# A transformer layer on one core: pre-norm weight applied behind the transposes, zeros through TensorE first, some masks by VectorE, a new order

## The chip, the core and the metric

The kernel runs on one core of a Trainium2 chip. A core has five engines with a queue of instructions each: TensorE (PE, matrix products and transposes), VectorE (DVE), ScalarE (ACT), GpSimd (POOL) and SyncE (SP, which here issues all DMAs). They run side by side and wait for each other by semaphores. TensorE reads SBUF and writes PSUM, which has eight banks of 128 x 512 float32. The metric is the device time of one execution in microseconds.

## The reference

One layer over 1024 tokens of width 1024, all in float32:

```python
h = rms_norm(x, norm_pre_g[i])          # x * rsqrt(mean(x*x) + EPS) * g
proj = h @ w_in[i]
# sb_q, sb_k, sb_v, sb_g, c_q, c_kv, k_rope, mla_g = split(proj)
# 8 heads of stick-breaking attention (strictly causal), head norm, times silu(sb_g)
# 8 heads of latent attention (low-rank q and kv, rotary key), head norm, times silu(mla_g)
y = concat([sb_y, mla_y]) @ w_out[i]
x = x + rms_norm(y, norm_post_g[i])
x = x + rms_norm(p[i] @ w_ple[i], ple_norm_g[i]) * sigmoid(x @ w_ple_gate[i] + b_ple_gate[i])
```

## The kernel before

Tokens come in eight tiles of 128 rows (x0 to x7). Every operand of a product is split into a high and a low part of the type fp32r, and a product of two operands is three TensorE products (high x high, high x low, low x high) summed in one PSUM bank.

**The head.** `HEAD` lists the first loads: four quarters of the weight of v (v0 to v3, each loaded and split by `load_split`), the tiles x0, x1, x2, and the pre-norm weight (g0, one row of 4 KB). Two products with a row of ones spread the weight over the 128 partitions, and ScalarE copies it to `gb["pre"]`. `x_norm(t)` squares and sums a tile (ScalarE), forms the mean (VectorE) and the power -1/2 (GpSimd), and multiplies the tile by both the power and the weight. `x_tr(t)` transposes it, four blocks of 128 x 128 to a bank, and `split` writes the high part (`hh`, ScalarE) and the low part (`hl`, VectorE). `token_proj(t)` then makes v for the tile: eight blocks kb with three products each; quarter i of the weight serves kb 2i and 2i+1. `xv_gen(t)` puts these together and loads x(t+3). The four first tiles are done ahead of everything else.

**The middle.** `SEQ` lists sixteen pairs of units: head pair c (0 to 3 stick-breaking, 4 to 7 latent), half s of the queries, and in each pair e = 0, 1. `sb_rows` makes the scores of four blocks of 128 queries: a product, a mask added on TensorE by a product of `eye` and `mask` (bf16, 128 columns), and a second product into the same bank; ScalarE reads the bank twice for two sigmoids. `Weaver` mixes projections (`FILL0`) into the units at `RATES`. `TAIL` lists the steps of the output projections at the end.

**The order.** Nothing is issued as it is written. `Recorder` records each operation with its dependences and a cost; `schedule` replays them through a model of the engines (`cost`, `LAT`) and takes, for each engine, the ready operation of lowest priority; `issue` emits the program in that order. The priority is `turn`, the operation's place in the program plus the first number of its piece in the table `SHIFT`; the second number ranks the requests for buffers. `R.piece` begins a new piece. `R.bias` shifts a stretch (`URGENT` for the head, `AHEAD` for scores). `FLIP` moves single operations between VectorE and GpSimd or ScalarE, `SPLITS` (read by `choice`) whole kinds of them between VectorE and GpSimd. Since all instructions are emitted in `issue`, the profile gives nearly all of them one line, L730; they are told apart by tiles: u and f are the two pools of SBUF slots, t and a the PSUM banks (five and three), h the large buffers, among them `hh` and `hl`.

Of the kernel before, what the change touches and what calls it, by code (L numbers as in the profile page):

```python
# [12 lines left out]
F32 = mybir.dt.float32  # L13
# [34 lines left out]
def f(ap):  # L48
# [6 lines left out]
TAIL = ("o4", "w1", "w2", "o5", "a4", "o6", "w3", "x1", "x0", "x2", "e4", "a0", "e0", "a6", "x3", "e6", "a2", "e2")  # L55
RATES = (4.934, 9.256, 4.735, 4.518, 3.1, 1.436, 0.789, 0.703, 2.078, 0.654, 0.413, 0.788, 0.259, 0.582, 0.786, 1.784)
URGENT = 56
EARLY = 4
LATER = 5
SEQ = ((0, 0), (1, 0), (6, 0), (4, 0), (7, 0), (2, 0), (0, 1), (3, 0), (3, 1), (2, 1), (5, 0), (7, 1), (5, 1), (4, 1), (1, 1), (6, 1))  # L60
FILL0 = ("x4", "x5", "l0", "x6", "x7", "q1", "c0", "b1", "r3", "t0", "lrv0", "g3", "rope0", "r0", "r1", "g4", "q2", "r2", "q3", "g6", "g0", "g1", "g2", "g7", "ple0", "g5")
# [4 lines left out]
SPLITS = (1, 0, 0, 1, 0, 1, 1, 1, 0, 1, 1, 1, 1, 1, 0, 1, 1, 0, 1, 0, 1, 1, 1, 0, 0, 1, 1, 1, 0, 0, 0, 1, 0, 0, 0, 1, 0, 0, 1, 0, 0, 1, 1)  # L66
HEAD = ("v0", "x1", "x0", "g0", "v3", "v1", "v2", "x2")
# [265 lines left out]
class Recorder:  # L333
# [127 lines left out]
    def cost(self, eng, op, args, kw, outs, aps, spaces):  # L461
        n = max(self.elems(a) for a in aps)
        ps = any(k == "psum" for _, k in spaces)
        if eng == "PE":
# [3 lines left out]
            if aps[1].dtype == BF16:  # L468
                return n * 0.305
# [47 lines left out]
    def schedule(self):  # L517
# [32 lines left out]
        dma_free = 0.0  # L550
        flight, room = [], 0
        port_free = 0.0
        table = None
        clock = {}

        why = self.why = {}
# [176 lines left out]
def block_kernel(ctx, tc, x, p, positions, norm_pre_g, w_in, q_norm_g, w_uq, kv_norm_g, w_ukv,  # L733
# [196 lines left out]
    gb = {}  # L930
# [857 lines left out]
```

## Time and profile before

| | |
|---|---|
| time, median of 3 runs | 773.64 us (772.73 to 775.02) |
| profiled execution: time, span | 774.4 us, 772.6 us |
| TensorE, VectorE, ScalarE, GpSimd busy | 98%, 81%, 50%, 45% |
| DMA traffic over the span | 148.69 MB, mean 192 GB/s |
| granted TensorE clock, mean | 0.998 |

The span runs from the first to the last instruction. A busy TensorE is not TensorE at its peak: ends of products are modelled, so a long row of products is best priced by its length over its count. A row of the chain of work gives start, length and what ran; a row of the groups gives count, then busy time and mean length in ns, then the idle time of the engine ahead of it and what ended that; a row of the timeline adds the engine and, in brackets, the idle time ahead.

### The profile page before, as it was taken

How to read it: one execution, taken by the hardware profiler on the slowest of the kernel's cores; microseconds unless marked ns; L12 is line 12 of the kernel's file. 1: busy time of each engine (PE TensorE's matmuls, PEld its weight loads, DVE VectorE, ACT ScalarE, POOL GpSimd, SP SyncE). 2: the span in 40 equal slices, each digit the busy share in tenths (PEclk: the TensorE clock that was granted, in tenths of full speed). 3: DMA queues.
4: the chain of work that ended last, by engine and by line, in shares of the span. 5: the costliest groups of instructions: out<-in, count | busy, mean ns of one | idle time of the engine just before them, and what ended most of it. 6: DMA issues, size and time to landing. Idle time of an engine off the chain costs nothing.

```text
span 772.6 us, 11778 instructions
## 1 busy us (share of the span) xinstructions
PE 754.5 (98%) x3912; PEld 621.5 (80%) x3912; DVE 624.1 (81%) x1184; ACT 384.9 (50%) x898; POOL 346.6 (45%) x315
## 2 busy tenths in 40 slices
PE   6999999999999999999999899999999999999997
PEld 4887889878788878888788788888888888778886
DVE  5876334499867877788888899999899998888996
ACT  6315123333443586565646768776776642433211
POOL 4445111102312258878884712342275114468664
PEclk9999999999999999999999999999999999999999
DMA  9644460269995844566356588686734475172242
GB/s 329 201 171 139 145 213 5 77 218 354 330 341 190 275 155 143 167 206 189 110 184 225 187 290 260 216 302 223 240 116 154 166 254 178 60 268 87 94 150 82
DMA packets 101966, 148.69 MB, mean 192 GB/s; under 512 B 7441, under 2 KB 55057, under 8 KB 101906
## 3 DMA queue, kind: packets, MB, share of 16 engines
q1 hardware_dynamic: 101906, 147.95, 57.4%
q8 instruction: 31, 0.51, 0.3%
q14 instruction: 29, 0.24, 0.1%
HBM read 101.26 MB, written 46.66 MB: 191 GB/s over the span
## 4 chain that ended last, share of the span: by engine, by line
PE 84%; DVE 7%; DMA 4%; ACT 2%; issue 1%; POOL 1%; SPq 1%; POOLq 0%; ACTq 0%; DVEq 0%
PE a L730 58%; PE t L730 26%; DVE u L730 4%; DVE f L730 2%; ACT u L730 1%; DMA u<-k_d 1%; DMA u<-in_w_ple_gate_dram 1%; DMA u<-q_d 1%; DMA u<-in_x_dram 1%; DMA f<-in_positions_dram 1%; DMA q_d<-f 1%; SPq L730 1%; DVE nm L730 1%; ACT f L730 0%; POOL u L730 0%
## 5 line engine op out<-in xcount | busy, mean ns | idle before, releaser
L730 POOL TENSOR_TENSOR u<-u,u 128x512 f32<-128x512 f32 (+16 forms) x134 | 200.5, 1512 | 153.3 <-DVE u L730 64.0
L730 PE MATMUL a<-h,f 128*128 128x512 f32 x864 | 242.1, 405 | 0.0
L730 PEld LDWEIGHTS a<-h,f 128*128 128x128 f32 x864 | 155.2, 189 | 26.8 <-DVE f L730 0.6
L730 DVE TENSOR_TENSOR u<-t,u 128x512 fp32r<-128x512 f32 (+4 forms) x284 | 150.6, 556 | 13.7 <-ACT u L730 10.0
L730 PE MATMUL t<-u,u 128*128 128x512 f32 (+4 forms) x580 | 154.4, 370 | 1.9 <-DMA u<-q_d 0.5
L730 PE MATMUL a<-u,u 128*128 128x512 f32 (+2 forms) x524 | 136.7, 371 | 0.5 <-DVE u L730 0.5
L730 PE MATMUL t<-ident,u 128*128 128x128 f32 x792 | 125.8, 276 | 2.4 <-DVE u L730 2.4
L730 ACT ACTIVATE u<-t 128x512 f32<-128x512 f32 (+5 forms) x208 | 91.0, 509 | 67.7 <-PE t L730 57.8
L730 PEld LDWEIGHTS t<-u,u 128*128 128x128 f32 x580 | 103.4, 189 | 23.2 <-DVE u L730 4.3
L730 ACT CAST u<-t 128x512 fp32r<-128x512 f32 (+3 forms) x187 | 85.6, 495 | 71.0 <-PE t L730 35.3
L730 PE MATMUL a<-h,u 128*128 128x512 f32 (+1 forms) x492 | 118.3, 390 | 0.4 <-DVE u L730 0.4
L730 PEld LDWEIGHTS t<-ident,u 128*128 128x128 f32 x792 | 97.8, 142 | 24.9 <-DVE u L730 7.0
L730 PEld LDWEIGHTS a<-h,u 128*128 128x128 f32 x492 | 90.0, 188 | 21.3 <-issue 1.0
L730 PEld LDWEIGHTS a<-u,u 128*128 128x128 f32 x524 | 93.1, 188 | 17.2 <-DVE u L730 2.2
L730 ACT ACTIVATE u<-t,nms 128x384 f32<-128x384 f32 (+4 forms) x96 | 55.3, 581 | 42.3 <-DVE nms L730 35.3
L730 DVE TENSOR_TENSOR_SCAN u<-u 128x64 f32<-128x64 f32 (+6 forms) x64 | 59.1, 934 | 20.6 <-ACT u L730 20.4
L730 DVE TENSOR_TENSOR u<-u,u 128x512 f32<-128x512 f32 (+13 forms) x91 | 73.2, 820 | 2.0 <-ACT u L730 1.1
L730 DVE TENSOR_TENSOR u<-a,u 64x512 f32<-64x512 f32 (+4 forms) x75 | 47.8, 649 | 15.6 <-ACT u L730 9.7
L730 DVE TENSOR_REDUCE nm<-t 128x1 f32<-128x384 f32 (+4 forms) x96 | 51.6, 545 | 2.1 <-PE t L730 1.3
L730 POOL TENSOR_TENSOR rs<-ms,nhalf 128x8 f32<-128x8 f32 x16 | 27.7, 1731 | 57.0 <-DVE ms L730 37.5
L730 ACT ACTIVATE f<-a 128x512 bf16<-128x512 f32 (+3 forms) x64 | 34.3, 538 | 36.7 <-PE a L730 32.1
L730 PE MATMUL a<-u,h 128*128 128x512 f32 x192 | 49.8, 406 | 0.0
(110 smaller groups left out, 795.5 us busy)
## 6 DMA issues: line engine op xcount, KB each, us to landing
u<-q_d SPq DMA_DIRECT2D x64, 256.0 KB, 4.7
u<-k_d SPq DMA_DIRECT2D x16, 512.0 KB, 5.3
u<-v_d SPq DMA_DIRECT2D x16, 512.0 KB, 4.5
u<-in_w_ple_gate_dram SPq DMA_DIRECT2D x16, 512.0 KB, 5.4
f<-in_w_in_dram SPq DMA_DIRECT2D x14, 512.0 KB, 5.0
v_d<-u SPq DMA_DIRECT2D x12, 512.0 KB, 4.1
f<-in_x_dram SPq DMA_DIRECT2D x9, 512.0 KB, 4.6
k_d<-u SPq DMA_DIRECT2D x9, 512.0 KB, 3.9
```

Of the source, the lines that this page charges most:

```text
L730: x["fn"](*[place(a) for a in x["args"]], **{k: place(a) for k, a in x["kw"].items()})
```

## The change

- The tables are new: `TAIL`, `RATES`, `SEQ`, `FILL0`, `SPLITS`, `HEAD`, `SHIFT`, `FLIP`.
- The pre-norm weight comes as a column: one load of eight rows of 128, one small transpose, a copy to `g_pre` (128 x 8). `x_norm` multiplies by the power alone, and `x_tr` applies the weight of each block kb when the bank is read: eight pairs of operations of 128 x 128 per tile instead of two pairs of 128 x 512. The broadcast weight and GpSimd's (or VectorE's) second multiply for x4 to x7 go.
- Twelve products of zeros (bf16, 512 columns) stand ahead of the head, and one power on GpSimd.
- In the units named by `BYDVE` (c, e, s of 0,0,0; 1,1,1; 2,0,0; 3,1,0) the mask is added by VectorE behind both products.
- The planner's model: a load reaches its user later, a bf16 product is dearer, a scale from memory costs ScalarE 60 ns, and two engines that read one bank do so one behind the other.

```diff
-EARLY = 4
+EARLY = 7
-HEAD = ("v0", "x1", "x0", "g0", "v3", "v1", "v2", "x2")
+HEAD = ("g0", "v0", "x0", "v1", "v2", "v3", "x2", "x1")
+GAINS = 8
+WARM = (12, 0)
+BYDVE = (1, 0, 0, 0, 0, 0, 0, 1, 1, 0, 0, 0, 0, 0, 1, 0)
 SHIFT = {
...
+    0: (1204, 1209), 1: (-381, -413), 2: (-586, -394), 3: (-857, -953), 4: (-1159, -1106), 5: (-11, -91),
+    6: (53, -44), 7: (121, 23), 8: (258, 2), 9: (-1185, -486), 10: (68, -288), 11: (-2224, -2216), 12: (21, -205),
+    13: (-51, -344), 14: (36, -130), 15: (-2, -127), 16: (160, -173), 17: (-127, -396), 18: (-376, -8),
...
 FLIP = (
+    22, 23, 29, 30, 32, 124, 182, 242, 298, 300, 305, 335, 360, 379, 433, 445, 451, 453, 515, 517, 523, 524, 526,
...
+        banks = [a.tensor.name for a, (w, k) in zip(aps[1:], spaces) if k == "psum"]
...
-                return n * 0.305
+                return n * 0.416
...
-           ("POOL", "DVE"): 65.0, ("POOL", "POOL"): 102.0, ("POOL", "SP"): 55.0, ("SP", "PE"): 650.0,
-           ("SP", "ACT"): 620.0, ("SP", "DVE"): 620.0, ("SP", "POOL"): 650.0, ("SP", "SP"): 620.0}
+           ("POOL", "DVE"): 65.0, ("POOL", "POOL"): 102.0, ("POOL", "SP"): 55.0, ("SP", "PE"): 950.0,
+           ("SP", "ACT"): 900.0, ("SP", "DVE"): 900.0, ("SP", "POOL"): 950.0, ("SP", "SP"): 900.0}
...
+                for key in x["banks"]:
+                    for y, t in read.get(key, {}).items():
+                        if y != e:
+                            s = max(s, t + LAT[y, e])
...
+    g_pre = const([128, 8], "g_pre")
+    still = const([128, 512], "still", BF16)
+    DVE.memset(still, 0.0)
+    rstd_warm = const([128, 1], "rstd_warm")
+    POOL.tensor_tensor(rstd_warm, hpi, nhalf[:, 0:1], ALU.pow)
...
-        if t < EARLY:
+        if t < GAINS:
             for v in half if t == 0 else [slice(0, D)]:
-                DVE.scalar_tensor_tensor(xt[:, v], xt[:, v], rs, gb["pre"][:, v], ALU.mult, ALU.mult)
+                DVE.tensor_scalar(xt[:, v], xt[:, v], rs, None, ALU.mult)
...
-            split(hh[t // 4][:, ks, sl], hl[t // 4][:, ks, sl], ps.rearrange("q (k n) -> q k n", k=4), heng=ACT)
...
+            for kb in range(4 * g, 4 * g + 4):
+                src, a = ps[:, kb % 4 * 128:kb % 4 * 128 + 128], hh[t // 4][:, kb, sl]
+                ACT.activation(a, src, AF.Copy, scale=g_pre[:, kb:kb + 1])
+                DVE.scalar_tensor_tensor(hl[t // 4][:, kb, sl], src, g_pre[:, kb:kb + 1], f(a), ALU.mult, ALU.subtract)
...
-            gb["pre"] = k4(dt=F32, name="gb_pre")
-            gb["row"] = k4(dt=F32, name="gb_row")
-            SP.dma_start(gb["row"][0:1], norm_pre_g[0:1, :])
+            gb["col"] = k2((128, 128), F32, "gb_col")
+            SP.dma_start(gb["col"][0:8], norm_pre_g[0].rearrange("(b q) -> b q", q=128))
...
+    R.bias = WARM[1]
+    idle = ps_a()
+    for _ in range(WARM[0]):
+        mm(idle, still[:, 0:128], still, start=True, stop=True)
+    R.bias = 0
...
-    for n in range(2):
-        ps = ps_t()
-        mm(ps, ones, gb["row"][0:1, half[n]], start=True, stop=True)
-        ACT.copy(gb["pre"][:, half[n]], ps)
+    ps = ps_t()
+    PE.transpose(ps[:, 0:8], gb["col"][0:8], ident[0:8, 0:8])
+    ACT.copy(g_pre, ps[:, 0:8])
...
-                if ks.stop == nk:
+                by_dve = BYDVE[4 * i[0] + 2 * i[1] + s]
+                if ks.stop == nk and not by_dve:
                     mm(ps[:, h - 128:h], eye, mask, start=False, stop=False)
                 mm(ps[:, 0:w], qb[:, qc], kk[:, kw], start=False, stop=True)
+                if ks.stop == nk and by_dve:
+                    DVE.tensor_tensor(ps[:, h - 128:h], ps[:, h - 128:h], mask, ALU.add)
```

With `GAINS = 8` all tiles take the new path; the old one (`gain`, `EARLY`) is left in the code and isn't reached.

More of the change, by code (lines that the diff above doesn't have):

```diff
@@ L54 @@
 TICK = 10240.0 / 3.0
-TAIL = ("o4", "w1", "w2", "o5", "a4", "o6", "w3", "x1", "x0", "x2", "e4", "a0", "e0", "a6", "x3", "e6", "a2", "e2")
-RATES = (4.934, 9.256, 4.735, 4.518, 3.1, 1.436, 0.789, 0.703, 2.078, 0.654, 0.413, 0.788, 0.259, 0.582, 0.786, 1.784)
+TAIL = ("w1", "o4", "w2", "x1", "o5", "a4", "w3", "o6", "x0", "e4", "a0", "x2", "x3", "e0", "a6", "e6", "a2", "e2")
+RATES = (4.934, 9.256, 4.735, 4.518, 2.716, 1.436, 0.789, 0.633, 2.078, 0.686, 0.349, 0.957, 0.19, 0.436, 0.903, 0.217)
 URGENT = 56
-EARLY = 4
+EARLY = 7
 LATER = 5
-SEQ = ((0, 0), (1, 0), (6, 0), (4, 0), (7, 0), (2, 0), (0, 1), (3, 0), (3, 1), (2, 1), (5, 0), (7, 1), (5, 1), (4, 1), (1, 1), (6, 1))
-FILL0 = ("x4", "x5", "l0", "x6", "x7", "q1", "c0", "b1", "r3", "t0", "lrv0", "g3", "rope0", "r0", "r1", "g4", "q2", "r2", "q3", "g6", "g0", "g1", "g2", "g7", "ple0", "g5")
+SEQ = ((0, 0), (1, 0), (6, 0), (4, 0), (7, 0), (2, 0), (0, 1), (3, 0), (3, 1), (2, 1), (5, 0), (7, 1), (4, 1), (5, 1), (1, 1), (6, 1))
+FILL0 = ("x4", "x5", "l0", "x6", "x7", "c0", "b1", "r3", "q1", "t0", "lrv0", "g3", "rope0", "g4", "r0", "r1", "q2", "r2", "g6", "q3", "g0", "g1", "g7", "g2", "ple0", "g5")
 N1 = 3
@@ L65 @@
 LOWS = ("g", "q", "ple", "x", "b", "c", "t", "l")
-SPLITS = (1, 0, 0, 1, 0, 1, 1, 1, 0, 1, 1, 1, 1, 1, 0, 1, 1, 0, 1, 0, 1, 1, 1, 0, 0, 1, 1, 1, 0, 0, 0, 1, 0, 0, 0, 1, 0, 0, 1, 0, 0, 1, 1)
-HEAD = ("v0", "x1", "x0", "g0", "v3", "v1", "v2", "x2")
+SPLITS = (1, 0, 0, 1, 0, 1, 1, 1, 0, 1, 1, 1, 0, 0, 0, 1, 1, 0, 0, 0, 1, 1, 0, 0, 0, 1, 1, 1, 0, 0, 1, 1, 1, 0, 1, 1, 1, 0, 1, 0, 0, 0, 0)
+HEAD = ("g0", "v0", "x0", "v1", "v2", "v3", "x2", "x1")
+GAINS = 8
+WARM = (12, 0)
+BYDVE = (1, 0, 0, 0, 0, 0, 0, 1, 1, 0, 0, 0, 0, 0, 1, 0)
 AHEAD = 52
 SHIFT = {
[151 rows of a table removed]
[160 rows of a table added]
 }
 FLIP = (
[12 rows of a table removed]
[11 rows of a table added]
 )
@@ L438, in add @@
         stored = eng == "SP" and spaces[-1][1] != "sbuf"
-        self.ins.append(dict(port=port, hold=525.0 if back else 420.0, descs=self.descriptors(aps, outs) if eng == "SP" else 0, lead=500.0 if stored else 1700.0, eng=eng, op=op, fn=fn, args=args, kw=kw, deps=deps, uses=set(uses), dur=dur,
+        self.ins.append(dict(port=port, banks=banks, hold=525.0 if back else 420.0, descs=self.descriptors(aps, outs) if eng == "SP" else 0, lead=500.0 if stored else 1700.0, eng=eng, op=op, fn=fn, args=args, kw=kw, deps=deps, uses=set(uses), dur=dur,
                              cols=self.columns(op, args) if eng == "PE" else 0,
@@ L474, in cost @@
             return n * 0.833 + (52 if any(k == "psum" and not w for w, k in spaces) else 93) \
-                + (93 if "accum_out" in kw else 0) + (93 if isinstance(kw.get("bias"), bass.AP) else 0)
+                + (93 if "accum_out" in kw else 0) + (93 if isinstance(kw.get("bias"), bass.AP) else 0) + (
+                    60 if isinstance(kw.get("scale"), bass.AP) else 0)
         if eng == "DVE":
@@ L553, in schedule @@
         table = None
+        read = {}
         clock = {}
@@ L674, in schedule @@
                 free[e] = end
+                for key in x["banks"]:
+                    read.setdefault(key, {})[e] = end
             done += 1
@@ L865, in x_norm, with gain @@
         rstd_pow(rs, ms)
-        if t < EARLY:
+        if t < GAINS:
             for v in half if t == 0 else [slice(0, D)]:
-                DVE.scalar_tensor_tensor(xt[:, v], xt[:, v], rs, gb["pre"][:, v], ALU.mult, ALU.mult)
+                DVE.tensor_scalar(xt[:, v], xt[:, v], rs, None, ALU.mult)
+        elif t < EARLY:
+            DVE.scalar_tensor_tensor(xt, xt, rs, gain(), ALU.mult, ALU.mult)
         else:
             DVE.tensor_scalar(xt, xt, rs, None, ALU.mult)
-            POOL.tensor_tensor(xt, xt, gb["pre"], ALU.mult)
+            POOL.tensor_tensor(xt, xt, gain(), ALU.mult)
+    def gain():
+        if "pre" not in gb:
+            with above():
+                gb["pre"], row = k4(dt=F32, name="gb_pre"), k4(dt=F32, name="gb_row")
+            SP.dma_start(row[0:1], norm_pre_g[0:1, :])
+            for v in half:
+                ps = ps_t()
+                mm(ps, ones, row[0:1, v], start=True, stop=True)
+                ACT.copy(gb["pre"][:, v], ps)
+        return gb["pre"]
     def x_tr(t):
@@ L880, in x_tr @@
             ks, sl = slice(4 * g, 4 * g + 4), slice(t % 4 * 128, t % 4 * 128 + 128)
-            split(hh[t // 4][:, ks, sl], hl[t // 4][:, ks, sl], ps.rearrange("q (k n) -> q k n", k=4), heng=ACT)
+            if t >= GAINS:
+                split(hh[t // 4][:, ks, sl], hl[t // 4][:, ks, sl], ps.rearrange("q (k n) -> q k n", k=4), heng=ACT)
+                continue
+            for kb in range(4 * g, 4 * g + 4):
+                src, a = ps[:, kb % 4 * 128:kb % 4 * 128 + 128], hh[t // 4][:, kb, sl]
+                ACT.activation(a, src, AF.Copy, scale=g_pre[:, kb:kb + 1])
+                DVE.scalar_tensor_tensor(hl[t // 4][:, kb, sl], src, g_pre[:, kb:kb + 1], f(a), ALU.mult, ALU.subtract)
     def token_proj(ps, t, ws, n):
@@ L978, in c_gen @@
         c_tr(NT - 1, last)
+    R.piece("warm") if hasattr(R, "piece") else None
+    R.piece("warm")
+    R.bias = WARM[1]
[3 more added lines that the diff above has]
+    R.bias = 0
     for item in HEAD:
@@ L984, in block_kernel @@
     R.bias = -URGENT
-    for n in range(2):
-        ps = ps_t()
-        mm(ps, ones, gb["row"][0:1, half[n]], start=True, stop=True)
-        ACT.copy(gb["pre"][:, half[n]], ps)
+    ps = ps_t()
+    PE.transpose(ps[:, 0:8], gb["col"][0:8], ident[0:8, 0:8])
+    ACT.copy(g_pre, ps[:, 0:8])
     x_norm(0)
```

330 rows, old and new, of tables (FLIP, SHIFT) are left out of this document.

## The prediction

> **What bounds the kernel now.** I read the page's busy line and its chain first, then the chain in order of time, and last the busy time by stages.
>
> ```profile
> PE 754.5 (98%) x3912; PEld 621.5 (80%) x3912; DVE 624.1 (81%) x1184; ACT 384.9 (50%) x898; POOL 346.6 (45%) x315
> PE 84%; DVE 7%; DMA 4%; ACT 2%; issue 1%; POOL 1%; SPq 1%; POOLq 0%; ACTq 0%; DVEq 0%
> ```
>
> TensorE is busy 98% and carries 84% of the chain that ends last. So a change pays where TensorE has less work, starts sooner, or waits less.
>
> ```profile
> 2.12 5.62 DMA u<-in_x_dram
> 10.51 1.97 PE t L730 x8
> 12.47 1.04 PE a L730 x2
> 13.51 1.71 PE t L730 x8
> 15.22 8.20 PE a L730 x34
> 23.43 0.87 PE t L730 x8
> 736.61 28.14 PE a L730 x121
> 739.88 24.87 PE a L730 x107
> ```
>
> These rows of the chain give TensorE's price list and the head. A dense product of 512 columns takes 28.14/121 = 0.233 us, eight transposes 0.87 us. At 10.51 eight transposes took 1.97 us and two products 1.04: half speed. Dense work begins at 15.22, with 16 transposes and two products done, worth 2 x 0.87 + 2 x 0.233 = 2.2 us. So the **head loses 15.2 - 2.2 = 13.0 us**. The last product ends at 739.88 + 24.87 = 764.75; the tail behind it takes 7.85 us, and the change doesn't touch its last steps.
>
> ```profile
> 32.00:740.00 708.00, 701.78 (x3679) 579.82 (x3678) 577.71 (x1111) 360.96 (x859) 317.02 (x285) 1.00 0.58 193
> 32.00:100.00 68.00, 67.46 (x325) 54.17 (x324) 39.64 (x71) 19.84 (x45) 28.70 (x30) 1.00 0.47 161
> 400.00:600.00 200.00, 197.53 (x1109) 164.83 (x1108) 184.84 (x391) 142.06 (x345) 83.06 (x79) 1.00 0.66 219
> ```
>
> Columns: window, length, then busy time of PE, PEld, DVE, ACT, POOL. From 32 to 740 us TensorE is idle for 6.2 us in all, 2.5 of them at 400 to 600, where VectorE is busy 92%. So a new order can win at most about 6 us in the middle.
>
> **The head, part by part.**
>
> ```profile
> 5.17 1.04 ACT L730 CAST u<-u 128x1024 fp32r<-128x1024 f32 x1 [3.16 <-DMA u<-in_w_in_dram]
> 6.30 2.35 POOL L730 TENSOR_TENSOR u<-u,u 128x1024 fp32r<-128x1024 f32 x1 [4.37 <-ACT u L730]
> 6.44 1.06 ACT L730 ACTIVATE u<-u 128x1024 bf16<-128x1024 f32 x1 [0.22 <-DMA u<-in_x_dram]
> 7.41 0.19 ACT L730 ACTIVATION_READ_ACCUMULATOR u<-u 128x1 f32 x1
> 7.63 0.15 DVE L730 TENSOR_SCALAR sm<-ss 128x1 f32<-128x1 f32 x1 [5.74 <-ACT u L730]
> 6.44 0.38 SPq L730 DMA_DIRECT2D u<-in_w_in_dram  x1
> 8.61 1.59 POOL L730 TENSOR_TENSOR sr<-sm,nhalf 128x1 f32<-128x1 f32 x2
> 9.10 0.69 DVE L730 CAST u<-u 128x1024 fp32r<-128x1024 f32 x1
> 12.88 1.22 DVE L730 TENSOR_TENSOR u<-u,u 128x1024 fp32r<-128x1024 f32 x1
> 16.98 1.03 ACT L730 CAST u<-u 128x1024 fp32r<-128x1024 f32 x1
> L730 DVE TENSOR_SCALAR f<-f,hsr 128x1024 f32<-128x1024 f32 x8 | 5.9, 733 | 0.3 <-POOL hsr L730 0.3
> L730 DVE SCALAR_TENSOR_TENSOR u<-u,sr,u 128x1024 f32<-128x1024 f32 x3 | 3.8, 1275 | 0.0
> ```
>
> Loads come first: the first blocks land by 5.17 (v0), 6.44 (x0) and, by the chain, 2.12 + 5.62 = 7.74 (x1), 1.3 us apart. The rank of a load is its place in the program plus its SHIFT. By hand this gives the old order v0, x0, g, x1, v1, v2, x2, x3, x4, v3; the issue of v3 as the tenth, at 6.44, bears it out. The new one is x2 (-1151), v0 (-1138), g (-837), x0 (13), v1, x4 (both 78), x3 (92), x1 (103), v2 (149), x5, x6, v3 (289). So x2 lands first, at 5.2, and x0 two blocks later, at 7.8.
>
> The path of x2: Square 1.06 + 0.19 and hand-overs to 6.5, mean 0.15 to 6.65, the power 1.59/2 = 0.8 to 7.6. No weight split stands ahead of the power any more (the two flips at v0 move its 2.35 us from GpSimd to VectorE; now the power of x0 waits from 7.78 to 8.61 behind it). The row's normalization needs no broadcast weight: a TENSOR_SCALAR of 0.73 instead of a 1.28, to 8.4. Four transposes, then the first small piece on ScalarE, first product near 9.7. With the 0.87 us of its transposes done, the loss would be 9.7 - 0.9 = 8.8 us, 4.2 less than now. That is the upper end.
>
> ```profile
> L730 ACT CAST u<-t 128x128 fp32r<-128x128 f32 x25 | 7.1, 284 | 9.8 <-DVE u L730 6.5 <-PE t L730 3.2
> L730 ACT CAST h<-t 128x512 fp32r<-128x512 f32 x12 | 6.9, 588 | 11.3 <-PE t L730 11.3
> L730 DVE SCALAR_TENSOR_TENSOR f<-a,csr,f 128x128 f32<-128x128 f32 x8 | 2.7, 342 | 0.0
> L730 DVE TENSOR_TENSOR h<-t,h 128x512 fp32r<-128x512 f32 x16 | 10.8, 681 | 1.4 <-ACT h L730 1.4
> L730 POOL TENSOR_TENSOR u<-u,u 128x1024 f32<-128x1024 f32 x2 | 5.3, 2632 | 2.1 <-DVE u L730 2.1
> ```
>
> Against it stand the pieces. Per x tile VectorE now does 2 x 0.681 = 1.36 us behind the transposes; then 8 x 0.342 = 2.74. ScalarE goes from 2 x 0.588 = 1.18 to 8 x 0.284 = 2.27. GpSimd loses a multiply of up to 2.63 us for each of x4 to x7, off the chain. To feed the first 24 products VectorE must do: v0's low half 1.22, x2 0.73 + 2.74, x0 the same, v1 0.69 + 1.22 (all four wv splits leave GpSimd): 10.1 us from 6.5, so until 16.6. (1.22 and 0.69 are the rows at 12.88 and 9.10.) TensorE's own work in that time is 24 x 0.233 + 2 x 0.87 = 7.3 us from 9.7, until 17.0. VectorE just keeps up, and the pieces come in small steps, so I give back 1.7 us: **head -2.5 us, between 0 and -4.2**. The late v3 doesn't bind: its cast came at 16.98, two blocks of 1.3 us later is 19.6, and with 2.4 us for its halves 22.0; three open banks hold 54 products and 24 transposes, 15.2 us of work, until 24.9.
>
> The products on zeros use an idle TensorE. They wait only for a memset behind the eye cast on VectorE, so from about 2.3. Half speed lasted 4.7 us here, from 10.51 to 15.22; nine zeros of 0.52 us (1.04/2 above; these are bf16, it is the nearest row) and three of half that end at 2.3 + 4.7 + 0.8 = 7.8, in no one's way. If they don't count as work for the clock, they cost nothing and bring nothing. Their worth is inside the 4.2: 16 transposes at 0.87 per eight instead of 1.97 and 1.71 save 1.9 us. The first GpSimd power showed no start cost (two took 1.59), so the warm-up power saves nothing.
>
> The Trainium skill, page "TensorE: Matmul & The Clock Gate", section "What's actually happening", says that TensorE reaches full clock after about 3.4 us of work and drops back after an idle window of the same length. The half-speed rows at 10.51 agree, though the profile's own clock column shows 1.00 there; by that rule zeros that end too soon before the first transposes are worth nothing.
>
> **The masks.**
>
> ```profile
> L730 PE MATMUL t<-mask,eye 128*128 128x128 bf16 x64 | 14.7, 229 | 0.0
> 74.63 0.39 PE L730 MATMUL t<-u,u 128*128 128x512 f32 x1
> 74.86 0.23 PE L730 MATMUL t<-mask,eye 128*128 128x128 bf16 x1
> 74.90 0.47 PE L730 MATMUL t<-u,u 128*128 128x512 f32 x1
> 75.22 0.62 PE L730 MATMUL a<-u,h 128*128 128x512 f32 x2
> L730 DVE TENSOR_TENSOR u<-t,u 128x128 fp32r<-128x128 f32 x40 | 11.3, 281 | 2.6 <-ACT u L730 2.5
> ```
>
> Starts tell a product's price better than its 229 ns: the mask holds TensorE 0.04 us, and the product behind it takes 75.22 - 74.90 = 0.32 instead of 0.233. Together 0.13 us. BYDVE names four of sixteen units with four rows each, so 16 of the 64 go: **-2.0 us**, on the bounding engine. VectorE gets 16 x 0.281 = 4.5 us. Each add stands between the scores and two sigmoids and makes a row's path longer by 0.28 + 2 x 0.12 = 0.52 us (0.12 is a hand-over, below). The scores' 52 places of lead (AHEAD) hide it; without that cover it is 16 x 0.52 = 8.3 us.
>
> **The order.** It is planned anew with dearer loads (900 to 950 ns for 620 to 650) and with reads of one bank by two engines set apart.
>
> ```profile
> 661.84 0.60 ACT L730 ACTIVATE f<-a 128x512 bf16<-128x512 f32 x1 [0.94 <-PE a L730]
> 662.56 0.69 DVE L730 TENSOR_TENSOR f<-a,f 128x512 f32<-128x512 f32 x1 [0.94 <-ACT f L730]
> ```
>
> VectorE needs nothing that this Square writes, and yet starts only 0.12 us behind its end: the chip's program already takes the readers of a bank in turn, and the old plan didn't know. A plan that knows should wait less; the middle has 6.2 us to give, and an unlucky order can take as much. I take **-1.5 us, from -5 to +5**.
>
> Sum: -2.5 - 2.0 - 1.5 = -6.0 us. The profiled execution took 774.4 us (span 772.6 and 1.8 around it), 0.76 above the median of 773.64. 774.4 - 6.0 - 0.76 = 767.6 us.
>
> **The rivals.** (A) The clock closes again before real work: the zeros are over by 7.8 or sooner, and the first transposes wait until 8.6 or, with VectorE late, 10. Then the 1.9 us above return: 767.6 + 1.9 = 769.5. For it: nothing behind the zeros is ready by 7.8. Against: the gap is only 1 to 2 us.
>
> (B) The pieces take turns at their bank: each of 16 hand-overs costs 0.12 us, and nothing overlaps: 8 x (0.284 + 0.342) + 16 x 0.12 = 6.9 us per tile, against 2 x (0.588 + 0.12 + 0.681) = 2.8 now and 24 x 0.233 + 0.87 = 6.5 of TensorE's work. The first tile is 4.1 later, three more 0.4 each: 5.3, against the head's 4.2; with the masks' 2.0 and the order's 1.5 it is 773.64 + 1.1 - 3.5 = 771.2, and about 773 if the order gains nothing. Against it: the tile has two banks, so ScalarE can work in one while VectorE is in the other. The Trainium skill, page "PSUM — Partial Sum Buffer", section "PSUM bank collisions raise a hardware error", says that reads of one bank by two engines collide and must be kept apart by waits; the row at 662.56 shows such a wait.
>
> (C) VectorE becomes the bound. It gets 8 x (2.74 - 1.36) = 11.0 us of pieces, 4.5 of masks, and is spared 4 x 0.54 = 2.2: +13.3 us of 624. Early there is room (28 us idle from 32 to 100), late hardly (15 us idle in 400 to 600). Where it has none, each microsecond shows; from 6 us that show, the gain is gone; with 9.5 of the 13.3: 773.64 - 6.0 + 9.5 = 777.1, slower.
>
> **Chances.** My forecast 0.52 (763.5 to 771); A 0.15; B 0.20, which I count as no change; C 0.13. A change of 0.3%, 2.3 us, is about what can be told from none. Faster 0.67, same 0.20, slower 0.13. The range leaves out most of C and a windfall in the order: 763.5 to 776.
>
> **What would show it.** Right: the first full-speed product near 10 us and dense work by 12; transposes at 0.87 per eight from the start; 48 mask products; idle of TensorE from 32 to 740 not above 6. Wrong: transposes at twice 0.87 (A); DVE and ACT alternating with idle in the head and dense work only from 15 (B); TensorE waiting for "DVE u" at 400 to 600 with VectorE over 95% (C).

## The result, and the profile after

| | before | after |
|---|---|---|
| time, median of 4 runs each | 774.33 us (772.73 to 775.71) | 766.83 us (765.48 to 768.41) |
| profiled execution: time, span | 774.4 us, 772.6 us | 765.48 us, 763.7 us |

The ratio is 0.9905, with a 95% interval of 0.9875 to 0.9934: faster by 7.5 us, about 1%. The forecast was 767.6 us, 6.0 less than the 773.64 of then. The total came out within 0.8 us of it, but its terms were of the wrong size, and their errors cancelled in part. One execution of the changed kernel in its second set of times, at 1910.82 us, is slow, and the ratios leave it out.

The busy line and the chain of the profile after, engine by engine:

```profile
PE 751.0 (98%) x3905; PEld 621.0 (81%) x3905; DVE 630.6 (83%) x1238; ACT 399.7 (52%) x962; POOL 321.7 (42%) x306
PE 88%; ACT 5%; DVE 3%; DMA 2%; issue 1%; POOL 0%; SPq 0%; ACTq 0%; DVEq 0%; POOLq 0%
```

TensorE now carries 88% of the chain instead of 84%, and its busy share is 98% as before. So the gain can't be read from the share; it has to be looked for stage by stage. First the busy time by stages of the kernel before (window, length, then PE, PEld, DVE, ACT, POOL with their counts, the granted clock, the share of the DMA engines, GB/s):

```profile
32.00:400.00 368.00, 364.89 (x1889) 300.92 (x1888) 265.84 (x523) 167.75 (x412) 166.72 (x158) 1.00 0.58 191
400.00:450.00 50.00, 47.76 (x261) 38.98 (x260) 44.75 (x84) 34.73 (x86) 28.94 (x29) 1.00 0.63 209
450.00:740.00 290.00, 289.13 (x1532) 239.92 (x1531) 267.13 (x505) 158.48 (x362) 121.36 (x99) 1.00 0.58 194
```

The same stages of the kernel after:

```profile
32.00:400.00 368.00, 367.20 (x1914) 306.32 (x1913) 277.82 (x551) 184.28 (x459) 164.13 (x162) 1.00 0.58 194
400.00:450.00 50.00, 48.12 (x267) 38.90 (x266) 44.72 (x105) 34.65 (x88) 28.13 (x26) 1.00 0.70 229
450.00:740.00 290.00, 289.04 (x1512) 241.13 (x1512) 264.77 (x492) 153.75 (x350) 113.39 (x93) 1.00 0.56 189
```

From 32 to 400 us TensorE was idle for 3.11 us and now for 0.80, and it got 25 more products through in that time. At 400 to 450, where both kernels wait most, nothing is gained. And the head, in TensorE's timeline of the kernel after (start, length, what, count, idle time ahead):

```profile
2.21 5.24 PE L754 MATMUL a<-still 128*128 128x512 bf16 x12 [2.21 <-DVE still L754]
7.38 1.25 PE L754 MATMUL t<-ident,u 8*128 8x8 f32 x9
9.17 1.61 PE L754 MATMUL a<-u,h 128*128 128x512 f32 x5 [0.54 <-ACT h L754]
10.81 1.09 PE L754 MATMUL t<-ident,u 128*128 128x128 f32 x8
12.80 4.76 PE L754 MATMUL a<-u,h 128*128 128x512 f32 x19 [0.90 <-ACT h L754]
17.81 1.09 PE L754 MATMUL t<-ident,u 128*128 128x128 f32 x8 [0.24 <-DVE sm L754]
```

The zeros run into the first transposes, which go at full speed (1.25 us for eight and the small one). The trace's own record of the clock agrees: its first stretch of full clock starts at 7.26 us here, and at 15.78 in the kernel before. (Ahead of the first stretch on record the views print 1.00 whatever the speed; that is the 1.00 which the prediction saw beside the half-speed rows.) The first product starts at 9.17 and dense work at 12.80, where before it was 15.22.

**A ledger of lost time.** Busy times hide small losses, since the ends of products are modelled. Starts are better. I went through each trace from one TensorE product to the next, subtracted from the step between their starts the price that a product of its shape has in dense rows (0.232 us for 512 columns, 0.118 for 256, 0.109 for a transpose, others between; zeros, rows of ones and masks at nothing), and added up what remains. The priced work is 729.35 us in every kernel here, so the span is 729.35 plus these losses, in us; "masks" holds each mask and what it delays behind it:

| profile | span | head, 0–32 | masks | 32–400 | 400–450 | 450–740 | tail |
|---|---|---|---|---|---|---|---|
| before | 772.6 | 13.19 | 7.73 | 8.99 | 3.51 | 4.37 | 5.46 |
| before, a second profile | 773.3 | 11.87 | 7.71 | 9.93 | 3.61 | 5.41 | 5.46 |
| after | 763.7 | 10.95 | 5.78 | 3.78 | 4.28 | 4.34 | 5.22 |
| after, a second profile | 765.8 | 10.82 | 6.02 | 3.95 | 4.24 | 6.16 | 5.24 |

By the means of the two profiles each: head -1.6, masks -1.8, 32 to 400 -5.6, 400 to 450 +0.7, 450 to 740 +0.4, tail -0.2; together -8.2 us. **Most of the gain lies at 32 to 400 us**, where the prediction had put the smallest of its terms.

### The profile page after: what moved, and what is told of

Read it like the earlier page. It is cut to its first block, busy times and chain, and to the rows that moved or that the text cites. A ratio compares the mean times of both kernels' runs of the same rounds, so it can differ in the third digit from the quotient of the medians.

```text
span 763.7 us, 11831 instructions
## 1 busy us (share of the span) xinstructions
PE 751.0 (98%) x3905; PEld 621.0 (81%) x3905; DVE 630.6 (83%) x1238; ACT 399.7 (52%) x962; POOL 321.7 (42%) x306
## 4 chain that ended last, share of the span: by engine, by line
PE 88%; ACT 5%; DVE 3%; DMA 2%; issue 1%; POOL 0%; SPq 0%; ACTq 0%; DVEq 0%; POOLq 0%
PE a L754 62%; PE t L754 26%; ACT u L754 3%; DVE u L754 1%; DMA u<-k_d 1%; DMA v_d<-f 1%; ACT L754 1%; ACT h L754 1%; ACT f L754 1%; DVE nm L754 1%; DVE f L754 1%; DMA u<-v_d 0%; SPq L754 0%; DVE t L754 0%; DVE nms L754 0%
## 5 line engine op out<-in xcount | busy, mean ns | idle before, releaser
L754 POOL TENSOR_TENSOR u<-u,u 128x512 f32<-128x512 f32 (+14 forms) x134 | 190.5, 1436 | 140.1 <-ACT u L754 74.8
L754 PE MATMUL t<-u,u 128*128 128x512 f32 (+4 forms) x580 | 151.0, 367 | 1.0 <-DMA u<-k_d 0.5
L754 PE MATMUL t<-ident,u 128*128 128x128 f32 (+1 forms) x793 | 126.4, 273 | 1.4 <-DVE nms L754 0.5
L754 PEld LDWEIGHTS t<-ident,u 128*128 128x128 f32 (+1 forms) x793 | 97.1, 140 | 22.3 <-DVE u L754 2.9
L754 DVE TENSOR_TENSOR u<-u,u 128x512 fp32r<-128x512 f32 (+8 forms) x88 | 79.6, 917 | 5.3 <-ACT u L754 3.5
L754 ACT ACTIVATE u<-t,nms 128x384 f32<-128x384 f32 (+5 forms) x96 | 55.2, 581 | 39.7 <-DVE nms L754 39.4
L754 DVE TENSOR_TENSOR_SCAN u<-u 128x320 f32<-128x320 f32 (+4 forms) x64 | 64.6, 1011 | 13.6 <-ACT u L754 12.4
L754 ACT ACTIVATE f<-a 128x512 bf16<-128x512 f32 (+2 forms) x64 | 34.2, 539 | 51.5 <-PE a L754 48.4
L754 POOL MEMSET u<- 128x128 f32 x64 | 13.0, 216 | 102.1 <-PE a L754 56.4
L754 DVE TENSOR_REDUCE nm<-t 128x1 f32<-128x384 f32 (+5 forms) x96 | 51.8, 547 | 1.9 <-PE t L754 1.2
```

The source lines that it names most:

```text
L754: x["fn"](*[place(a) for a in x["args"]], **{k: place(a) for k, a in x["kw"].items()})
```

## Experiments

All are edits of the kernel after unless another is named. Those of the type "in `issue`" leave the planned order as it is, so that only one thing differs. The first number is a median; ratios are against the kernel before, run on the same chip.

**The kernels again.** Two marks to read the others by: the kernel after, and the kernel before in one more execution, for a second profile of each.

> The changed kernel once more, as the mark for the three beside it: 766 to 768 us, 7 to 8 us under before.

> The kernel before once more, for a second profile of it: TensorE's lost time by stages within 1 us of the first profile where it is a property of the order, and apart where it is chance.

After again took 767.28 us, ratio 0.9893 (0.9868 to 0.9917); before again 775.11. Their rows are in the ledger. What they add: without any edit the head of the kernel before differs by 1.3 us between two profiles, and the stage 450 to 740 of the kernel after by 1.8. The head is seen in TensorE's timeline of the second profile of before:

```profile
10.23 2.04 PE L730 MATMUL t<-ident,u 128*128 128x128 f32 x8 [0.53 <-DVE u L730]
12.02 1.22 PE L730 MATMUL a<-u,h 128*128 128x512 f32 x2
13.04 1.20 PE L730 MATMUL t<-ident,u 128*128 128x128 f32 x8
13.99 8.14 PE L730 MATMUL a<-u,h 128*128 128x512 f32 x34
```

The second eight transposes took 1.20 us, not the 1.71 of the first profile's chain: here the clock is full from 13.36 on instead of 15.78, and dense work began at 13.99. So a single profile of a head can't settle a difference under about 1 us.

### The head

**No zeros.** The twelve products on zeros are left out; nothing else moves.

```diff
-            for i in order:
+            for i in (j for j in order if not any(isinstance(a, bass.AP) and "still" in a.tensor.name
+                                                  for a in self.ins[j]["args"][1:])):
```

> The changed kernel without the twelve products on zeros; every other instruction in the same order. If the zeros open the clock for the first transposes, as the forecast had it, the transposes at 7 us run at half speed and the time rises by 1 to 2 us. If the head is bound by ScalarE's small pieces anyway (rival), TensorE's half speed hides behind them: within 0.5 us, or 0.3 us faster, since the first transposes no longer stand behind the zeros (7.45 us).

It took 766.06 us, ratio 0.9882 (0.9863 to 0.9901): no slower than with them. TensorE's timeline without the zeros:

```profile
6.94 1.97 PE L754 MATMUL t<-ident,u 128*128 128x128 f32 x8 [1.13 <-DVE u L754]
9.22 2.50 PE L754 MATMUL a<-u,h 128*128 128x512 f32 x5 [0.31 <-ACT h L754]
11.52 1.91 PE L754 MATMUL t<-ident,u 128*128 128x128 f32 x8
13.08 4.96 PE L754 MATMUL a<-u,h 128*128 128x512 f32 x19
```

The zeros do open the clock: without them it is full only from 13.73 us, and eight transposes take 1.97 us instead of some 1.1, five products 2.50 instead of 1.61, eight more transposes 1.91 instead of 1.09. Yet dense work begins at 13.08 instead of 12.80. All but 0.3 us of the faster TensorE was spent waiting, as the idle times of 0.54 and 0.90 "<-ACT h" in the timeline with zeros show: ScalarE's queue sets the pace. It does so from its first piece on. The Square of x0 stands ahead of the pieces of x2, and it waits for x0's load; without zeros:

```profile
7.76 1.06 ACT L754 ACTIVATE u<-u 128x1024 bf16<-128x1024 f32 x1 [1.02 <-DMA u<-in_x_dram]
```

With zeros the Square starts at 7.71, in the second profile of the kernel after at 7.59 (0.61 us behind the same load), and the first products follow at 9.22, 9.17 and 9.05. The transposes of x2 began at 6.94 (half speed), 7.45 and 6.91 (full speed): ready early or late, they wait for the same queue. Whether that Square behind the pieces would help wasn't tried. ScalarE's timeline of the kernel after in that stretch:

```profile
7.71 1.06 ACT L754 ACTIVATE u<-u 128x1024 bf16<-128x1024 f32 x1
8.77 0.61 ACT L754 ACTIVATE h<-t,g_pre 128x128 fp32r<-128x128 f32 x2
9.79 1.66 ACT L754 ACTIVATE h<-t,g_pre 128x128 fp32r<-128x128 f32 x6 [0.42 <-DVE h L754]
11.31 1.09 ACT L754 ACTIVATE u<-u 128x1024 bf16<-128x1024 f32 x1
12.35 0.92 ACT L754 ACTIVATE h<-t,g_pre 128x128 fp32r<-128x128 f32 x3
13.69 1.40 ACT L754 ACTIVATE h<-t,g_pre 128x128 fp32r<-128x128 f32 x5 [0.42 <-DVE h L754]
```

But for two waits of 0.42 it has no gap from 7.71 to 15.1: the Squares of the second and third tile (1.06 and 1.09) stand in line with the sixteen pieces of the first two.

**x2 later.** The first two loads are exchanged, so that v0 goes ahead of x2; nothing else moves.

```diff
+            sp = [k for k, i in enumerate(order) if self.ins[i]["eng"] == "SP"]
+            order[sp[0]], order[sp[1]] = order[sp[1]], order[sp[0]]
             for i in order:
```

> The changed kernel with its first two loads exchanged: the weight quarter v0 first, the tile x2 second, 1.3 us later; all else in the same order. If the first tile's path leads the head, dense work on TensorE begins 1 us or more later than 12.8 us and the time rises by 1 us. If ScalarE's row of small pieces and squares leads it (rival), what comes behind x0 is unmoved: under 0.4 us.

It took 768.3 us, ratio 0.9911 (0.9894 to 0.9927), some 1.0 to 1.5 more than the kernel after, though the intervals overlap. The Square of x2 starts at 6.49 instead of 4.13. TensorE's timeline:

```profile
2.21 4.48 PE L756 MATMUL a<-still 128*128 128x512 bf16 x12 [2.21 <-DVE still L756]
6.62 0.22 PE L756 MATMUL t<-ident,u 8*128 8x8 f32 x1
9.30 1.97 PE L756 MATMUL t<-ident,u 128*128 128x128 f32 x8 [2.45 <-DVE u L756]
10.94 2.16 PE L756 MATMUL a<-u,h 128*128 128x512 f32 x5
14.57 4.73 PE L756 MATMUL a<-u,h 128*128 128x512 f32 x19 [0.60 <-ACT h L756]
```

Dense work begins at 14.57, 1.8 us later; the load order is worth that much, the half speed that it brings on included. The row at 9.30 shows rival A's mechanism. The twelve zeros took 4.48 us, so the last of them ran at full speed; TensorE then was idle for 2.45 us, and the transposes took 1.97, half speed again; by the record the clock is halved from 9.13 to 12.55 us.

**Weight ahead of the transposes.** `GAINS = 0` takes all tiles back to the old path of the weight (spread by rows of ones, multiplied into the tile before it is transposed), with the new load order, zeros, tables and masks. The order is planned anew, so only the first 32 us are read.

```diff
-GAINS = 8
+GAINS = 0
```

(The index by which `SHIFT` and `FLIP` look up an operation is corrected for the operations that come and go, so that the tables still name the same ones.)

> The changed kernel with the pre-norm weight multiplied in ahead of the transposes as before (spread by two products with ones, 512-wide splits), with the new order of loads and the zeros; planned anew, so only the first 32 us are to be read. If the small pieces on ScalarE and VectorE hold the head up, as my give-back of 1.7 us said, TensorE's dense work begins earlier than 12.8 us. If the spreading of the weight holds it (rival), the first transposes come later than 7.5 us and dense work no earlier.

It took 794.19 us (one execution); its later stages suffer from the new plan, as in the section on the order. TensorE's timeline of the head:

```profile
7.34 1.25 PE L755 MATMUL a<-still 128*128 128x512 bf16 x5
8.52 0.22 PE L755 MATMUL t<-ident,u 8*128 8x8 f32 x1
10.41 1.97 PE L755 MATMUL t<-ident,u 128*128 128x128 f32 x8 [1.67 <-DVE u L755]
12.20 2.50 PE L755 MATMUL a<-u,h 128*128 128x512 f32 x5
14.50 1.69 PE L755 MATMUL t<-ident,u 128*128 128x128 f32 x8
15.95 4.01 PE L755 MATMUL a<-u,h 128*128 128x512 f32 x16
```

With x2 loaded first and zeros issued, the first transposes still start at 10.41, as in the kernel before (10.51), and dense work at 15.95. The head loses 13.21 us against 10.95: 2.3 us more, and the early load and the zeros bring nothing in this plan. In the old path the tile waits for the weight's way over load, rows of ones and copy. Part of the 2.3 us may belong to this plan, though, which puts the Square of x2 behind the first copy of the weight on ScalarE; in the kernel after it starts at 4.13:

```profile
7.06 1.06 ACT L755 ACTIVATE u<-u 128x1024 bf16<-128x1024 f32 x1
```

How much the old path would cost with the Square first wasn't tried. Again five zeros at full speed (0.25 us each), 1.67 us of idle time, and transposes at half speed.

### The masks

**Back on TensorE.** The sixteen adds on VectorE become products of `eye` and `mask` again, each at the place in the order that the add had. Its time was taken twice, beside 775.55 and 774.03 us of the kernel before.

```diff
+                if (x["eng"] == "DVE" and x["op"] == "tensor_tensor" and isinstance(x["args"][2], bass.AP)
+                        and x["args"][2].tensor.name == self.mask.tensor.name):
+                    self.mm(place(x["args"][0]), self.eye, self.mask, start=False, stop=True)
+                    continue
...
-                mm(ps[:, 0:w], qb[:, qc], kk[:, kw], start=False, stop=True)
+                mm(ps[:, 0:w], qb[:, qc], kk[:, kw], start=False, stop=not (ks.stop == nk and by_dve))
```

> The changed kernel with its sixteen VectorE mask adds made products on TensorE again, each in the place of the add; everything else in the same order. If TensorE's time is the price (0.04 us and 0.08 us at the product behind it), the time rises by 16 x 0.12 = 2 us. If VectorE's relief of 16 x 0.28 = 4.5 us counts as much (rival), it is unchanged or 1 us faster.

> The kernel with the sixteen masks on TensorE once more, beside the one without them: by TensorE's price it is 1 to 2 us slower than that, by the first such run (no change) equal.

They took 766.78 us, ratio 0.9891 (0.9868 to 0.9914), and 767.63 us, ratio 0.9910 (0.9894 to 0.9926). The kernel after, beside the first of them, had 0.9893. The ledger's masks rise from 5.78 and 6.02 to 6.99 in both: 1.1 us for sixteen, less than the 0.12 us of each mask before (7.73/64). The starts show why: the price depends on what stands behind the mask.

```profile
65.50 0.23 PE L755 MATMUL t<-mask,eye 128*128 128x128 bf16 x1
65.54 0.48 PE L757 MATMUL a<-u,h 128*128 128x512 f32 x1
271.99 0.23 PE L755 MATMUL t<-mask,eye 128*128 128x128 bf16 x1
272.05 0.28 PE L757 MATMUL t<-ident,u 128*128 128x128 f32 x1
```

At 65.50 the next start but one is at 65.86: mask and product take 0.36 us, 0.13 more than the product's 0.232. Ten of the sixteen stand so, ahead of a product of 512 columns. The other six stand ahead of a transpose. At 271.99 the next start but one is at 272.09: mask and transpose take 0.10 us, where a lone transpose between wide products takes 0.03, so the mask costs 0.07. (The ledger prices that transpose at 0.109 and so makes these six too cheap.) Together that is 10 x 0.12 + 6 x 0.07 = 1.6 us. The time doesn't follow: what undoing costs lies within about 1 us of nothing.

**Adds left out.** The sixteen adds are dropped; these units are then not masked.

```diff
-            for i in order:
+            for i in (j for j in order if not (self.ins[j]["eng"] == "DVE" and self.ins[j]["op"] == "tensor_tensor"
+                                               and self.ins[j]["args"][2].tensor.name == self.mask)):
```

> The changed kernel with the sixteen VectorE mask adds left out, so that these rows see keys that they must not see; all else in the same order. If the adds are hidden behind TensorE, as the forecast had it, the time is that of the changed kernel within 0.5 us. If they lie on waits of TensorE (rival), it falls by 1 to 3 us.

It took 767.03 us, ratio 0.9904 (0.9888 to 0.9921): the adds cost nothing that can be measured, as forecast. That it is the scores' lead which covers them fits, but no run takes the lead away.

**All masks on VectorE.** The other 48 are turned into adds too, directly behind the second product of their block, at places that the planner didn't choose.

```diff
+                key = x["args"][0].tensor.name
+                if x["op"] == "matmul" and x["args"][1].tensor.name == self.eye.tensor.name:
+                    held[key] = x["args"][0]
+                    continue
...
+                if x["op"] == "matmul" and x["kw"]["stop"] and key in held:
+                    ps = place(held.pop(key))
+                    self.add_(ps, ps, self.mask, ALU.add)
```

> The changed kernel with the other 48 masks added by VectorE too, each behind its second product; all else in the same order. By TensorE's price of 0.12 us a mask the time falls by 48 x 0.12 = 5.8 us. By what the masks put back on TensorE showed (no change) it is within 1 us; where VectorE is 92% busy (400 to 600 us) its 48 x 0.28 = 13.5 us may show in part: up to 5 us slower.

It took 776.39 us, ratio 1.0016 (0.9999 to 1.0032): TensorE is rid of the last 5.8 us of masks, and the kernel is some 9 us slower than after, which is beyond all that was expected. The ledger of this run, against the first profile of after: masks 0 (5.78), 32 to 400 14.52 (3.78), 400 to 450 6.33 (4.28), 450 to 740 7.41 (4.34). The added adds in the groups, and the middle of the kernel in the busy time by stages:

```profile
L762 DVE TENSOR_TENSOR t<-t,mask 128x128 f32<-128x128 f32 x48 | 13.7, 292 | 9.2 <-PE t L759 8.3 <-ACT u L759 0.3
```

```profile
200.00:400.00 200.00, 195.43 (x1040) 159.44 (x1039) 163.86 (x326) 118.16 (x277) 121.67 (x113) 1.00 0.64 208
```

The kernel after in the same stretch:

```profile
200.00:400.00 200.00, 199.88 (x1096) 165.02 (x1095) 163.65 (x299) 121.35 (x282) 127.95 (x117) 1.00 0.63 208
```

TensorE loses 4.5 us in these 200 and gets 56 products fewer through. VectorE isn't full there: it is busy for 163.86 us against 163.65 (over the whole kernel its work rises from 630.6 to 642.4 us). It stands idle for 9.2 us ahead of these adds, 8.3 of them for a product, with work queued behind. That points to the place of a waiting instruction in VectorE's queue more than to its load. A rival isn't ruled out: the add makes the way from the scores to the sigmoids longer, and no run moves these adds to other places. Either way, what TensorE is spared (0.12 us a mask) is little beside it.

### The order

**A nudge of the planner's model.** One hand-over in `LAT`, VectorE to TensorE, is raised from 256 to 270 ns, in the kernel after and in the kernel before. If the order is good because the model is good, so small an error should hardly matter; if the tables were fitted to this very model, it matters much.

```diff
-           ("DVE", "PE"): 256.0
+           ("DVE", "PE"): 270.0
```

> The changed kernel planned anew with one hand-over of the planner's model (VectorE to TensorE) at 270 ns instead of 256, its tables unchanged. The model is hardly worse, but the order differs in half of its places. If the order's gain is the better model, the time stays within 1 us. If it is the fit of the tables to one exact plan (rival), it rises by 3 us or more.

> The kernel before, planned anew with the hand-over of 270 ns instead of 256, its own tables. If tables fit one plan only, it loses like the changed kernel did (33 us): 10 us or more. If only the changed kernel is that sensitive (rival), it stays within 3 us.

After with the nudge took 800.41 us, ratio 1.0325 (1.0305 to 1.0346), 33 us more than without; before with it 790.03, ratio 1.0188 (1.0171 to 1.0206), 15 us more. The loss of the first lies late: 10.37 at 400 to 450 (4.28) and 32.81 at 450 to 740 (4.34), with the head and 32 to 400 as they were (10.97 and 3.79), since the order of TensorE's products is nearly the same to there: of its first 1900 products, up to 375 us, 41 places hold one of another tile or shape. The busy time by stages of the nudged kernel late:

```profile
600.00:660.00 60.00, 53.94 (x265) 43.18 (x264) 45.60 (x96) 24.39 (x61) 12.16 (x12) 0.94 0.40 132
660.00:680.00 20.00, 13.24 (x45) 10.03 (x45) 11.09 (x16) 2.61 (x6) 10.43 (x7) 0.74 0.71 255
```

and the kernel after without it:

```profile
600.00:660.00 60.00, 59.79 (x307) 49.33 (x306) 54.57 (x92) 21.06 (x52) 22.77 (x16) 1.00 0.57 198
```

At 660 to 680 TensorE is idle for a third of the time and the granted clock is down to 0.74: a long wait there seems to cost a second time, by the clock. The waits of 600 to 700 of the nudged kernel (us in total, times, longest) name ScalarE and VectorE:

```profile
PE t L754 <- ACT u L754: 6.3, 4, 4.3
PE a L754 <- DVE u L754: 3.5, 2, 2.5
```

**The bank rule off.** The planner no longer sets the reads of one bank by two engines apart; the order is planned anew by the rest of the new model.

```diff
-                            s = max(s, t + LAT[y, e])
+                            pass
```

> The changed kernel planned without the rule that readers of a bank take turns, its tables unchanged; the chip's program still waits. If the rule carries the order's gain, TensorE's idle time rises in the stretches where ScalarE and VectorE share banks, 3 to 10 us. If any other plan of these tables loses (rival), the loss is of the size of the nudged plan, 20 to 40 us, in the same stretches (400 to 450, 600 to 700 us).

It took 803.58 us, ratio 1.0361 (1.0342 to 1.038). Its late loss, 31.64 at 450 to 740, is about that of the nudge (32.81), so it says nothing of the rule: a plan that keeps the rule loses as much there. Its loss at 32 to 400 is 8.59, that of the kernel before (8.99 and 9.93) and not that of after (3.78 and 3.95). There the nudge is no control, since it left the order nearly alone. The runs that keep the order (no zeros, x2 later, masks back on TensorE or left out) lose about 3 to 4.5 us there, like the kernel after. So the gain of 5.6 us at 32 to 400 belongs to the new order and goes without the rule; whether it goes because of the rule, or because any other plan there would lose it, is not settled. The run with the weight ahead of the transposes keeps the rule and is planned anew from the start, and it loses about 6.9 there, so about half of the gain went with the rule in force; but its operations differ too. What would tell it apart is a small change of the model that alters the order ahead of 400 us and keeps the rule; it wasn't tried.

## Why the prediction was right, and where it was wrong

**The bound.** TensorE bounds the kernel, and the change paid where TensorE started sooner or waited less: right. One reading was wrong. I took the point at which the chain leaves TensorE, 764.75, for its last product. TensorE's timeline of before goes on:

```profile
759.58 7.86 PE L730 MATMUL a<-h,u 128*128 128x512 f32 x45
```

The last product ends at 767.4 and the tail behind it is 5.2 us, not 7.85. No term hung on it; the tail changed by 0.2 us.

**Head, forecast -2.5, measured -1.6 (-2.2 by the first profiles).** The way is as forecast: x2 loaded first, the first product at 9.17 (near 9.7), the transposes near full speed from the start. That 9.7 was near is partly luck. x2 landed 1.1 us sooner than the 5.2 of the forecast (its Square starts at 4.13) and the power took 0.56 us, not 0.8, so the transposes could start at 6.9 and not at 8.4; what held the first product was ScalarE's queue with the Square of x0, which the forecast's path doesn't have. Dense work came at 12.80, not by 12, so the step that failed is the give-back, as to its engine. "VectorE just keeps up" was the reason given for it; it was ScalarE that didn't. The groups of the kernel after for the pieces on the two engines:

```profile
L754 DVE SCALAR_TENSOR_TENSOR h<-t,g_pre,h 128x128 fp32r<-128x128 f32 x64 | 17.6, 343 | 4.2 <-ACT h L754 4.0
L754 ACT ACTIVATE h<-t,g_pre 128x128 fp32r<-128x128 f32 x64 | 17.6, 396 | 2.8 <-PE t L754 1.9 <-DVE h L754 0.8
```

VectorE stood idle for 4.0 us for ScalarE ahead of its 64 pieces, ScalarE 0.8 for VectorE. The lengths of single pieces (343 and 396 ns, for 342 and 284 in the forecast) aren't what the queues pay, since pieces overlap: both engines were busy for 17.6 us with 64, 0.275 each. So ScalarE's sum was right, by way of the row of a plain cast, and VectorE's was too large (2.2 us for a tile, not 2.74). I counted VectorE's work up to the first 24 products but not the Squares of the next tiles on ScalarE, about 1.1 us each, which stand in the same queue.

**Zeros, "worth 1.9 us inside the 4.2": wrong.** They open the clock as assumed and are worth 0.3 us, since ScalarE's queue, from x0's load on, doesn't keep up. Nor were they in no one's way: in the first profile they ended at 7.45, and the transposes were ready at 6.9. The 1.9 were the sum of what TensorE's own rows became shorter by, and it was not asked what is late next.

**Masks, forecast -2.0; right in TensorE's rows, not shown in the time.** Between the two kernels the rows of the masks fall by 1.8 us, about as worked out. Putting sixteen back adds 1.6 in the rows and nothing measurable in the time, so the time shows no more than about 1 us of the 2.0. The hidden 4.5 us of adds were right: leaving them out gave no gain.

**Order, forecast -1.5 (-5 to +5), measured -5.6 at 32 to 400 us and +1.1 behind: mis-sized by 3 us**, inside its range. The bound "about 6 us in the middle" was read from idle time of records with modelled ends. By starts, the old order lost 9 to 10 us at 32 to 400 and 17 to 19 from 32 to 740. The place was wrong too: I looked at 400 to 600 us, where nothing came.

**The rivals.** A did not happen in the kernel after, where at most 0.90 us of idle time lay between zeros, transposes and products and the clock stayed full from 7.26 to 761.6 us; with x2 later or the weight ahead it does. B happens at single places (the two waits of 0.42 us "<-DVE h" above), 0.8 us of ScalarE's time ahead of 64 pieces instead of 16 hand-overs for each tile. The Trainium skill, page "PSUM — Partial Sum Buffer", section "PSUM bank collisions raise a hardware error", demands that reads of one bank by two engines be ordered; those two waits agree. C did not come: VectorE's busy time rose by 6.5 us (630.6 from 624.1), not by 13.3. The pieces were forecast at 11.0 us more and took 6.8 (17.6 for 10.8), and four casts of 128 x 512 from the same banks (2.7 us), which VectorE did before, are gone; what the new `SPLITS` and `FLIP` moved besides wasn't added up. The kernel with all masks on VectorE lost time with VectorE far from full.

So the forecast of the time was right with some luck: the head and the masks brought 1 to 2 us less than forecast, and the order 3 us more.

## What to carry to other kernels

Before you price the warming of an engine, or any shortening of its own rows, ask which engine feeds it next; here TensorE rows that were to save 1.9 us gave 0.3. Where the bounding engine is nearly always busy, measure its loss by the steps between starts, stage by stage, and not by idle time: the idle time here hid most of what a better order could give. And an order found by a planner belongs to its model: an error of 14 ns in one of its numbers cost 15 and 33 us, so changes to such a kernel are compared with the order held fixed.

## What the runs showed of the hardware

- The clock fell back to half in two heads, and its record moves in steps of 3.41 us. With x2 later (first two rows) it is full from 5.72 to 9.13 us and half to 12.55; with the weight ahead (last two) it is full from 5.59 to 9.00 and half to 15.83:

```profile
5.72:9.13 3.41, 1.13 (x6) 0.36 (x4) 0.79 (x2) 2.64 (x5) 0.56 (x1) 1.00 1.03 402
9.13:12.55 3.42, 3.25 (x12) 2.86 (x13) 2.69 (x7) 2.17 (x8) 0.55 (x1) 0.50 1.02 410
5.59:9.00 3.41, 3.15 (x10) 1.04 (x9) 0.15 (x1) 2.42 (x5) 0.52 (x1) 1.00 0.93 335
9.00:15.83 6.83, 5.42 (x20) 4.54 (x21) 6.73 (x10) 5.24 (x11) 0.96 (x2) 0.50 1.03 413
```

  So the idle times of 2.45 and 1.67 us ahead of the slow transposes are no threshold. In the second case the clock fell at 9.00, 0.26 us behind the last small transpose. In the 3.41 us ahead of each fall TensorE was busy, for 1.13 and for 3.15 us; the 3.15 hold products of a single row of ones until 7.40. Why they didn't hold the clock is open. The Trainium skill, page "TensorE: Matmul & The Clock Gate", section "What's actually happening", gives an idle window of about 3.4 us for the drop. The length agrees with these steps; that the window was idle doesn't, and here the measurement decides.
- A mask product of 128 columns cost 0.12 us ahead of a product of 512 columns and 0.07 ahead of a lone transpose.
- A piece of 128 x 128 read from a bank with a scale from memory takes ScalarE 396 ns, and a new one starts every 0.28 us (64 keep it busy for 17.6 us).
